# Output projection restaged: norm factor applied at each head's end, first weight chunks fetched early into idle buffers, transposes one block later

## The chip, the cores and the metric

The kernel runs on one core of a Trainium2 chip. The metric is device time in microseconds (us) of one execution. A core has a matrix engine (TensorE, "PE" in the profile, with its weight loads as "PEld"), a vector engine ("DVE"), a scalar engine for activations ("ACT"), GpSimd ("POOL"), and SyncE ("SP"), which here issues every DMA, in one order. All engines run side by side, each through its own fixed list of instructions, and wait for one another by semaphores. Data lies in DRAM, in on-chip SBUF of 128 partitions, and in PSUM banks, into which PE writes.

## The reference

A decoder trunk of two layers, 1024 tokens by 1024 features, with 256 memory tokens. Each layer projects the normalised input into the columns of several branches, mixes them into 2048 channels, gates them, and projects back with a residual:

```python
def layer(x, ...):
    u = rms_norm(x, norm_g) @ w_in          # split by columns into branches
    y = concat(branches(u)) * silu(z)       # 2048 channels
    return x + y @ w_out                    # the output projection

# layer 0: differential attention (8 heads, ALiBi), gated causal conv (512 ch.), memory attention (4 heads)
attn = p1 - lam * p2
o = einsum('bhqk,bhkd->bhqd', attn, v)
o = rms_norm(o, out_g) * (1.0 - lam_init)   # the norm factor: over a head's 128 channels, one per token
conv = b_gate * conv_w3(c_gate * h)
# layer 1: forgetting attention (12 heads) and memory attention (4 heads)
```

## The kernel before, in words

Every matrix product of the projections, of the scores and of attention with v is made of three float32r matmuls (high times high, high times low, low times high); `split` (L124) makes a high part on ACT and a low part on DVE or POOL. Tile rings decide reuse: `pool.tile(..., tag=t, bufs=n)` takes the next of the n buffers of tag t in program order, and its first writer waits until the last reader of the tile that lay there is done. A scheduler turns the program into one fixed order for each engine; two calls of `high_priority` pull attention and PSUM evacuation forward in it.

**Layer 0** runs the eight differential heads (`diff_head`, `diff_attend` L489), with a convolution group (`conv_group`, L534) spread over every two heads, then two pairs of memory heads (`x_pair`, `x_attend`), then `out_proj` (L735). Weights against the features come in two kinds: token units (`token_unit`, L187 to L191: q, k, v in token rows) and feature units (`feature_unit`, L218 to L220: gates and the convolution's four products in feature rows). Both write to the three PSUM banks of tag "d" (`pd`); scores use "s" (2), transposes "t" (2), and attention times v together with the sums of squares share one bank "o". The order lays these projections of the next head between the attention steps of this one.

In a head, `diff_attend` goes through four groups of two query blocks (`gorder` 3, 2, 1, 0): biased scores with a running maximum (L394), exponentials, e1 - lam e2 (L510 on POOL, L511 on DVE), transposes, attention times v, then y = o times gain times gate (L516), stored to `y_dr` by groups (128 KB each); the squares of o are summed by a matmul with ones (`psm`, L524) and stored as a row of `ms_dr`. At the head's end the row is loaded, `rstd` (L116, on POOL) makes the norm factor, and the factor goes to `on_dr` (L531). It is not applied there but in `out_blocks` (L702), to the stored y: four blocks of 128 channels by 128 tokens are loaded as `yr`, the factors as `rn`, broadcast over partitions, and POOL multiplies (L717).

The convolution's third product, `post_b` (L553 to L556), needs a `pd` bank and a work tile `cv` of tag "hs"; tag "hs" of pool `pa` has three buffers, used by `cv`, `zz`, `th` (the tanh of a gate), `xr` and `rs`.

`out_proj` has two halves of 512 output columns. Half 0 takes pairs of token blocks, with split weights in the buffers of u (the transposed input, no longer needed), loaded and split by the first pair; half 1 takes block after block, with weights in tiles `wo` of the pool `p2`, which were loaded during half 0. `yr`, `rn` and the raw weights share tag "raw" (4 buffers) of `pa`. At the end of each block of half 1 in layer 0 the row block of h is completed, normalised for the next layer (`norm_block`, L130) and transposed by PE into the next u (L141). Pool `p2` is opened after the branch's pools `p1` and `pw` and lies in their memory.

Of the kernel before, what the change touches and what calls it, by code (L numbers as in the profile page):

```python
# [7 lines left out]
F32 = mybir.dt.float32  # L8
F32R = mybir.dt.float32r
# [6 lines left out]
P = 128  # L16
# [17 lines left out]
class Trunk:  # L34
    def __init__(self, ctx, tc, io):
# [4 lines left out]
        self.pa = ctx.enter_context(tc.tile_pool(name="pa", bufs=1))  # L40
        self.st = ctx.enter_context(tc.tile_pool(name="st", bufs=4))
# [17 lines left out]
        self.queue, self.groups, self.boot = [], 0, True  # L59
# [70 lines left out]
    def norm_block(self, src, gb, xn, dst_hi, dst_lo):  # L130
# [5 lines left out]
        nc.vector.scalar_tensor_tensor(out=xn, in0=src, scalar=r, in1=gb, op0=ALU.mult, op1=ALU.mult)  # L136
        for j in range(2):
# [6 lines left out]
            while o < 4:  # L144
                (h, n), (l, _) = dst_hi.pop(0), dst_lo.pop(0)
                self.split(h, l, tv[:, o:o + n, :], nc.vector)
                o += n

# [29 lines left out]
    def token_unit(self, weights, lhs_hi, lhs_lo, nblk, post, together=False):  # L178
# [5 lines left out]
        for t0 in range(0, nblk, step):  # L184
# [7 lines left out]
            for tb, ps, _, _ in blks:  # L192
                with self.tc.high_priority(PRIO_EVAC):
                    post(tb, ps)
            self.tick()
# [29 lines left out]
    def gate_unit(self, w, c0, own=None):  # L225

        nc = self.nc
        if own is None:
            gate = {half: self.p1.tile([P, 512], F32, name="gate", tag="gate", bufs=2) for half in (1, 0)}
# [67 lines left out]
    def att_half(self, name):  # L297
        return self.p1.tile([P, 512], F32R, name=name, tag=name, bufs=self.attb)
# [10 lines left out]
    def mem_norm(self, layer, mem, g):  # L309
        nc = self.nc  # L310
        gb = self.p1.tile([P, T + 4], F32, name="mgb", tag="c1", bufs=1)[:, :D]
# [7 lines left out]
        for b in range(2):  # L319
            x = self.p1.tile([P, T], F32, name="mx", tag="E1", bufs=self.e1b)  # L320
            nc.sync.dma_start(out=x, in_=mem[b * P:(b + 1) * P, :])
            xn = self.p1.tile([P, T], F32, name="mxn", tag="bias", bufs=1)
# [166 lines left out]
    def diff_attend(self, h, maps, vh, vl, gate):  # L489
        nc = self.nc  # L490
        bias = self.bias
        nc.vector.tensor_scalar(out=bias, in0=bias, scalar1=0.5, scalar2=None, op0=ALU.mult)
        for g in self.gorder:
# [21 lines left out]
            y = self.pa.tile([P, 256], F32, name="y", tag="y", bufs=2)  # L515
            nc.vector.scalar_tensor_tensor(out=y, in0=o, scalar=self.g_o, in1=gate[g], op0=ALU.mult, op1=ALU.mult)  # L516
            self.emit_y(0, h, g, y)
# [13 lines left out]
        nc.sync.dma_start(out=self.on_dr[h].rearrange("(p b) -> p b", b=8), in_=self.rstd(ms, 8, "on"))  # L531


    def conv_group(self, g, w):  # L534

        nc = self.nc
        ch = self.p1.tile([P, T + 4], F32, name="ch", tag="c1", bufs=1)
# [109 lines left out]
    def fox_head(self, h, w):  # L647
# [13 lines left out]
        ck = self.p1.tile([P, T], F32, name="ck", tag="bias", bufs=1)  # L661
# [40 lines left out]
    def out_blocks(self, layer, tbs, half, tiles, res, fetch=None):  # L702
# [4 lines left out]
        for j in range(4):  # L707
            if fetch is not None:
                fetch(range(4 * j, 4 * j + 4))
            for tb, ps in zip(tbs, pss):  # L710
                ts = slice(tb * P, (tb + 1) * P)
                yr = self.pa.tile([P, 4, P], F32, name="yr2", tag="raw", bufs=4)
                nc.sync.dma_start(out=yr, in_=self.y_dr[layer][j * 512:(j + 1) * 512, ts].rearrange("(c p) t -> p c t", p=P))
                if layer == 0 and j < 2:
                    rn = self.pa.tile([P, 4, P], F32, name="rn", tag="raw", bufs=4)
                    nc.sync.dma_start(out=rn, in_=self.on_dr[4 * j:4 * j + 4, ts].unsqueeze(0).broadcast_to([P, 4, P]))
                    nc.gpsimd.tensor_tensor(out=yr, in0=yr, in1=rn, op=ALU.mult)  # L717
# [15 lines left out]
    def out_proj(self, layer, w, res, dst, g_next):  # L733
        nc, tc = self.nc, self.tc
        with tc.tile_pool(name=f"p2_{layer}", bufs=1, reuse_waits="tile") as p2:  # L735

            self.new_u()
            u = self.u
            w0 = lambda part, c: u[part][c // 8][:, c % 8, :]
            ws = [[p2.tile([P, 512], F32R, name=f"wo{p}_{c}") for c in range(16)] for p in range(2)]  # L740
            w1 = lambda part, c: ws[part][c]
            for tbs in ((tb, tb + 1) for tb in range(0, NB, 2)):
                fetch = (lambda cs: self.out_weights(w, 0, w0, cs, self.raw_tile)) if tbs[0] == 0 else None
                for tb, (ps, rs) in zip(tbs, self.out_blocks(layer, tbs, 0, w0, res, fetch)):
                    nc.vector.tensor_tensor(out=rs, in0=ps, in1=rs, op=ALU.add)
                    nc.sync.dma_start(out=dst[tb * P:(tb + 1) * P, :512], in_=rs)
                    raws = lambda: p2.tile([P, D], F32, name="wraw", tag=("hb", "xn")[tb % 2], bufs=2)[:, :512]
                    self.out_weights(w, 1, w1, range(2 * tb, 2 * tb + 2), raws)

            if g_next is not None:  # L750
                gb = p2.tile([P, D], F32, name="gb2")
                nc.sync.dma_start(out=gb, in_=g_next.broadcast_to([P, D]))
                self.new_u()
            for tb in range(NB):
                ts = slice(tb * P, (tb + 1) * P)
                hb = p2.tile([P, D], F32, name="hb", bufs=2)
                xn = p2.tile([P, D], F32, name="xn", bufs=2)
# [87 lines left out]
```

## Time and profile before

| | us |
|---|---|
| median of 3 runs | 2254.02 (2252.79 to 2254.55) |
| profiled execution, own time | 2251.72 |
| its span | 2249.9 |
| output projection 0 and the tail of the memory heads (from the last feature matmul of layer 0 to the last projection matmul) | 912.4 to 1172.0 |
| the same in layer 1 | 2053.4 to 2246.2 |

The profile is of one execution. Its page gives the busy time of each engine, the chain of work that ended last, and groups of instructions by line and shape; windows give the same between two times, and the timeline single instructions with the idle time before them and what ended it. A row such as "line engine op out<-in xcount | busy, mean ns | idle before, releaser" names the tile written, the tiles read, how often, and what the engine waited for.

### The profile page before, as it was taken

What the parts mean: (1) busy time and instruction counts of PE and PEld (TensorE: products, weight loads), DVE (VectorE), ACT (ScalarE), POOL (GpSimd) and SP (SyncE); (2) the same over time, 40 slices, a digit from 0 to 9 for tenths busy, and PEclk for the clock granted to TensorE, in tenths of its full rate; (3) what the DMA queues carried; (4) which work ended last, traced back from release to release, by engine and by line L of the source; (5) the groups of instructions that cost most, each with busy time, mean ns of one, the idle gap of its engine ahead of it and who ended that gap; (6) DMA issues with size and microseconds to landing.
All of it is one profiled execution on the core that took longest, in us unless ns stands there. A gap on an engine that the chain in (4) does not pass through costs nothing. (4 is left out here: it accounts for less than half of the span.)

```text
span 2249.9 us, 35841 instructions
## 1 busy us (share of the span) xinstructions
PE 2182.4 (97%) x12528; PEld 1974.7 (88%) x12528; DVE 1233.4 (55%) x2860; ACT 1057.8 (47%) x2503; POOL 1018.3 (45%) x1356
## 2 busy tenths in 40 slices
PE   7999999999999999888889999999999999999999
PEld 6889989889899899766679999999999999997887
DVE  5646756666665666542334555555555555555532
ACT  5655555465464554432234444444444444544421
POOL 4565655555555552332235555445555554522100
PEclk9999999999999999999999999999999999999999
DMA  5450210210201111585552221121222211214753
GB/s 162 126 159 19 61 56 17 70 47 23 71 27 44 51 59 36 168 243 161 137 144 54 57 53 36 40 55 48 55 57 57 57 40 38 61 55 137 222 155 98
DMA packets 266076, 183.06 MB, mean 81 GB/s; under 512 B 24572, under 2 KB 242844, under 8 KB 265896
## 3 DMA queue, kind: packets, MB, share of 16 engines
q1 hardware_dynamic: 265896, 180.77, 28.3%
q8 instruction: 99, 1.62, 0.3%
q14 instruction: 81, 0.66, 0.1%
HBM read 153.32 MB, written 27.38 MB: 80 GB/s over the span
## 5 line engine op out<-in xcount | busy, mean ns | idle before, releaser
L189 PE MATMUL pd<-wqh,u 128*128 128x384 f32 (+2 forms) x1536 | 513.7, 335 | 0.6 <-ACT wqh L127 0.5
L190 PE MATMUL pd<-wql,u 128*128 128x384 f32 (+2 forms) x1536 | 512.1, 334 | 0.0
L191 PE MATMUL pd<-wqh,u 128*128 128x384 f32 (+2 forms) x1536 | 511.4, 333 | 0.0
L189 PEld LDWEIGHTS pd<-wqh,u 128*128 128x128 f32 x1536 | 290.2, 189 | 4.9 <-ACT u L127 0.8
L190 PEld LDWEIGHTS pd<-wql,u 128*128 128x128 f32 x1536 | 290.2, 189 | 4.9 <-POOL wql L128 0.2
L191 PEld LDWEIGHTS pd<-wqh,u 128*128 128x128 f32 x1536 | 290.0, 189 | 4.3
L220 PE MATMUL pd<-u,wfh 128*128 128x512 f32 x704 | 277.9, 395 | 0.0
L219 PE MATMUL pd<-u,wfl 128*128 128x512 f32 x704 | 277.5, 394 | 0.0
L218 PE MATMUL pd<-u,wfh 128*128 128x512 f32 x704 | 277.2, 395 | 0.0
L128 POOL TENSOR_TENSOR wql<-raw,wqh 128x384 fp32r<-128x384 f32 (+2 forms) x220 | 217.0, 997 | 89.0 <-ACT wqh L127 83.7
L258 DVE TENSOR_TENSOR qr<-qr,rs_r 128x256 f32<-128x256 f32 x200 | 137.3, 687 | 106.7 <-POOL rs_r L121 105.2
L127 ACT ACTIVATE yh<-yr 128x512 fp32r<-128x512 f32 x128 | 79.9, 629 | 235.4 <-POOL yr L717 124.2
L121 POOL TENSOR_TENSOR rs_r<-rs_v,neghalf 128x2 f32<-128x2 f32 (+2 forms) x220 | 177.7, 809 | 14.1
L127 ACT ACTIVATE pth<-pt 128x512 fp32r<-128x512 f32 (+1 forms) x232 | 121.9, 555 | 130.1 <-PE pt L411 128.0
L673 POOL TENSOR_TENSOR fbias<-ck,cqn 128x896 f32<-128x896 f32 (+3 forms) x96 | 110.3, 1149 | 156.4 <-DVE mx L394 123.6
L128 DVE TENSOR_TENSOR yl<-yr,yh 128x512 fp32r<-128x512 f32 x128 | 89.7, 706 | 164.0 <-ACT yh L127 158.3
L127 ACT ACTIVATE wqh<-raw 128x384 fp32r<-128x384 f32 (+2 forms) x256 | 118.4, 481 | 125.4 <-DMA raw<-in_e_w_in_dram 62.6
L128 POOL TENSOR_TENSOR wfl<-rawf,wfh 128x512 fp32r<-128x512 f32 x88 | 119.4, 1358 | 106.1 <-ACT wfh L127 105.8
L128 DVE TENSOR_TENSOR ptl<-pt,pth 128x512 fp32r<-128x512 f32 (+1 forms) x232 | 143.7, 639 | 42.9 <-ACT pth L127 40.8
L128 POOL TENSOR_TENSOR vl<-qr,vh 128x128 fp32r<-128x128 f32 x160 | 80.6, 510 | 175.0 <-ACT vh L127 168.0
L220 PEld LDWEIGHTS pd<-u,wfh 128*128 128x128 f32 x704 | 132.4, 188 | 27.3 <-issue 0.6
L219 PEld LDWEIGHTS pd<-u,wfl 128*128 128x128 f32 x704 | 132.4, 188 | 26.4 <-issue 1.4
(239 smaller groups left out, 4992.4 us busy)
## 6 DMA issues: line engine op xcount, KB each, us to landing
yr<-y_dr SPq DMA_DIRECT2D x128, 256.0 KB
raw<-in_o_w_in_dram SPq DMA_DIRECT2D x288, 64.0 KB
rawf<-in_e_w_in_dram SPq DMA_DIRECT2D x56, 256.0 KB
y_dr<-y SPq DMA_DIRECT2D x112, 128.0 KB
raw<-in_e_w_in_dram SPq DMA_DIRECT2D x192, 64.0 KB
wraw<-in_e_w_out_dram SPq DMA_DIRECT2D x32, 256.0 KB
rn<-on_dr SPq DMA_DIRECT2D x32, 256.0 KB
rawf<-in_o_w_in_dram SPq DMA_DIRECT2D x32, 256.0 KB
```

Source lines behind the costliest of these rows:

```text
L121: nc.gpsimd.tensor_tensor(out=r[:, :n], in0=v[:, :n], in1=self.neghalf[:, :n], op=ALU.pow)
L127: nc.scalar.activation(out=hi, in_=src, func=AF.Copy)
L128: lo_eng.tensor_tensor(out=lo, in0=src, in1=f32(hi), op=ALU.subtract)
L189: nc.tensor.matmul(ps[:, :n], lhsT=ah(k), rhs=h, start=(k == 0), stop=False)
L190: nc.tensor.matmul(ps[:, :n], lhsT=ah(k), rhs=l, start=False, stop=False)
L191: nc.tensor.matmul(ps[:, :n], lhsT=al(k), rhs=h, start=False, stop=(k == KC - 1))
L218: nc.tensor.matmul(ps, lhsT=h, rhs=uh[:, k, :], start=(k == 0), stop=False)
L219: nc.tensor.matmul(ps, lhsT=l, rhs=uh[:, k, :], start=False, stop=False)
L220: nc.tensor.matmul(ps, lhsT=h, rhs=ul[:, k, :], start=False, stop=(k == KC - 1))
L258: nc.vector.tensor_tensor(out=v, in0=v, in1=r.unsqueeze(2).broadcast_to([P, ng, gs]), op=ALU.mult)
L673: nc.gpsimd.tensor_tensor(out=b[:, :kext], in0=ck[:, :kext], in1=self.cqn[:, qb, h:h + 1].broadcast_to([P, kext]), op=ALU.subtract)
```

## The change

Three parts.

1. The differential heads keep y of the whole head in a tile `yt` (128 channels by 1024 tokens, 2 buffers). After the factor is stored to `on_dr`, two halves of it are loaded broadcast over the partitions into `rn`, now of tag "hs"; DVE multiplies `yt` by it, and SP stores each half of y (256 KB). The 32 loads of `rn` and multiplications on POOL in `out_blocks` go.
2. A pool `pk`, open for the whole kernel, holds the tags kd, kz, c1, bias and gate. `out_early` runs ahead of the last pair of memory heads and fetches and splits the first five of 16 weight chunks of half 0 into the buffers of kd, kz (three each), c1 and bias; the other eleven go to u as before.
3. `yr` has a tag of its own (5 buffers) in `p2`; the weights of half 1 come by `raw_tile`; half 1 of layer 0 loads the first half of its row block ahead of the matmuls, and normalises it in two steps: `norm_rows` at once, `turn_rows` (the transposes) behind the next block's matmuls, the last one in the first token unit of layer 1.

```diff
+        self.pk = ctx.enter_context(tc.tile_pool(name="pk", bufs=1))
...
+            if self.turn_last is not None:
+                self.turn_last()
+                self.turn_last = None
...
-            gate = {half: self.p1.tile([P, 512], F32, name="gate", tag="gate", bufs=2) for half in (1, 0)}
+            gate = {half: self.pk.tile([P, 512], F32, name="gate", tag="gate", bufs=2) for half in (1, 0)}
...
-        return self.p1.tile([P, 512], F32R, name=name, tag=name, bufs=self.attb)
+        pool = self.pk if name in ("kd", "kz") else self.p1
+        return pool.tile([P, 512], F32R, name=name, tag=name, bufs=self.attb)
...
+        yt = self.p1.tile([P, T], F32, name="yt", bufs=2)
...
-            y = self.pa.tile([P, 256], F32, name="y", tag="y", bufs=2)
-            nc.vector.scalar_tensor_tensor(out=y, in0=o, scalar=self.g_o, in1=gate[g], op0=ALU.mult, op1=ALU.mult)
-            self.emit_y(0, h, g, y)
+            nc.vector.scalar_tensor_tensor(out=yt[:, gs], in0=o, scalar=self.g_o, in1=gate[g], op0=ALU.mult, op1=ALU.mult)
...
+        for half in range(2):
+            cs = slice(half * 512, (half + 1) * 512)
+            rn = self.pa.tile([P, 512], F32, name="rn", tag="hs", bufs=3)
+            nc.sync.dma_start(out=rn, in_=self.on_dr[h:h + 1, cs].broadcast_to([P, 512]))
+            nc.vector.tensor_tensor(out=yt[:, cs], in0=yt[:, cs], in1=rn, op=ALU.mult)
+            nc.sync.dma_start(out=self.y_dr[0][h * P:(h + 1) * P, cs], in_=yt[:, cs])
...
-        ch = self.p1.tile([P, T + 4], F32, name="ch", tag="c1", bufs=1)
+        ch = self.pk.tile([P, T + 4], F32, name="ch", tag="c1", bufs=1)
...
+    def out_early(self, w):
+
+        early = [[], []]
+        for i in range(3):
+            for part, n in enumerate(("kd", "kz")):
+                early[part].append(self.att_half(n))
+        for t in ("c1", "bias"):
+            two = self.pk.tile([P, T + 4] if t == "c1" else [P, T], F32R, name="we", tag=t, bufs=1)
+            for part in range(2):
+                early[part].append(two[:, part * 512:(part + 1) * 512])
+        self.early = early
+        self.out_weights(w, 0, lambda part, c: early[part][c], range(len(early[0])), self.raw_tile)
...
-    def out_blocks(self, layer, tbs, half, tiles, res, fetch=None):
+    def out_blocks(self, layer, tbs, half, tiles, res, pool, fetch=None):
...
-                yr = self.pa.tile([P, 4, P], F32, name="yr2", tag="raw", bufs=4)
+                yr = pool.tile([P, 4, P], F32, name="yr2", tag="yr", bufs=5)
...
-                if layer == 0 and j < 2:
-                    rn = self.pa.tile([P, 4, P], F32, name="rn", tag="raw", bufs=4)
-                    nc.sync.dma_start(out=rn, in_=self.on_dr[4 * j:4 * j + 4, ts].unsqueeze(0).broadcast_to([P, 4, P]))
-                    nc.gpsimd.tensor_tensor(out=yr, in0=yr, in1=rn, op=ALU.mult)
...
-            u = self.u
-            w0 = lambda part, c: u[part][c // 8][:, c % 8, :]
+            u, early = self.u, self.early
+            ne = len(early[0])
+            w0 = lambda part, c: early[part][c] if c < ne else u[part][(c - ne) // 8][:, (c - ne) % 8, :]
...
-                fetch = (lambda cs: self.out_weights(w, 0, w0, cs, self.raw_tile)) if tbs[0] == 0 else None
-                for tb, (ps, rs) in zip(tbs, self.out_blocks(layer, tbs, 0, w0, res, fetch)):
+                fetch = (lambda cs: self.out_weights(w, 0, w0, [c for c in cs if c >= ne], self.raw_tile)) if tbs[0] == 0 else None
+                for tb, (ps, rs) in zip(tbs, self.out_blocks(layer, tbs, 0, w0, res, p2, fetch)):
...
-                    raws = lambda: p2.tile([P, D], F32, name="wraw", tag=("hb", "xn")[tb % 2], bufs=2)[:, :512]
-                    self.out_weights(w, 1, w1, range(2 * tb, 2 * tb + 2), raws)
+                    self.out_weights(w, 1, w1, range(2 * tb, 2 * tb + 2), self.raw_tile)
...
+            turn = None
...
-                xn = p2.tile([P, D], F32, name="xn", bufs=2)
-                ((ps, rs),) = self.out_blocks(layer, [tb], 1, w1, res)
+                if g_next is not None:
+                    nc.sync.dma_start(out=hb[:, :512], in_=dst[ts, :512])
+                ((ps, rs),) = self.out_blocks(layer, [tb], 1, w1, res, p2)
+                if turn is not None:
+                    turn()
                 nc.vector.tensor_tensor(out=hb[:, 512:], in0=ps, in1=rs, op=ALU.add)
                 nc.sync.dma_start(out=dst[ts, 512:], in_=hb[:, 512:])
                 if g_next is not None:
-                    nc.sync.dma_start(out=hb[:, :512], in_=dst[ts, :512])
-                    self.norm_block(hb, gb, xn, *self.u_dst(tb))
+                    t = ("bias", "c1")[tb % 2]
+                    xn = self.pk.tile([P, T + 4] if t == "c1" else [P, T], F32, name="xn2", tag=t, bufs=1)[:, :D]
+                    self.norm_rows(hb, gb, xn)
+                    turn = lambda xn=xn, tb=tb: self.turn_rows(xn, *self.u_dst(tb))
+            self.turn_last = turn
...
+                if pr == 1:
+                    self.out_early(io["e_w_out"][0])
```

What this does to the lists of instructions, at three places. The lines of "after" are twelve to eighteen numbers higher for the same code (L516 is L529, L553 to L556 are L571 to L574, L524 is L536, L218 to L220 are L230 to L232).

DVE at the third odd head (of eight, counted from 0, the head 5), before, around the first scores of head 5 (`e_7271` and `e_7272`; the y is head 4's last):

```order
L295 TENSOR_TENSOR kz<-pt,kd 64x256
L553 TENSOR_SCALAR cv<-ch,cw,cb 128x512 x2
L394 ISA e_7271,mxp<-pss,abias 128x512
L394 ISA mxp 128x1
L554 SCALAR_TENSOR_TENSOR cv<-ch,cw,cv 128x512 x2
L394 ISA e_7272,mxp<-pss,abias 128x512
L394 ISA mxp 128x1
L555 SCALAR_TENSOR_TENSOR cv<-ch,cw,cv 128x512 x2
L516 SCALAR_TENSOR_TENSOR y<-po,g_o,gate 128x256
L242 SCALAR_TENSOR_TENSOR gate<-th,pd 128x512
L394 ISA e_7271,mx<-pss,abias,mxp 128x384
L394 ISA mx 128x1
```

DVE in the changed kernel, at the end of head 5:

```order
L525 SCALAR_TENSOR_TENSOR e_7638<-e_7638,rl,e_7639 128x256
L529 SCALAR_TENSOR_TENSOR yt<-po,g_o,gate 128x256
L129 TENSOR_TENSOR ptl<-pt,pth 128x384
L529 SCALAR_TENSOR_TENSOR yt<-po,g_o,gate 128x256
L571 TENSOR_SCALAR cv<-ch,cw,cb 128x512
L572 SCALAR_TENSOR_TENSOR cv<-ch,cw,cv 128x512
L548 TENSOR_TENSOR yt<-yt,rn 128x512
L573 SCALAR_TENSOR_TENSOR cv<-ch,cw,cv 128x512
L548 TENSOR_TENSOR yt<-yt,rn 128x512
L571 TENSOR_SCALAR cv<-ch,cw,cb 128x512
L574 TENSOR_TENSOR ch<-cv,pd 128x512
```

The convolution's `cv` stood between the two heads and ahead of the scores of head 5; it now stands at the end of head 5, and the product that frees a `pd` bank (`ch<-cv,pd`) behind the two multiplications by `rn`.

PE before, around the last sum of squares (`psm`) of head 5; `u` and `wfh` or `wfl` are feature units, `pss` scores of the next head:

```order
L220 MATMUL pd<-u_99,wfh 128x512
L218 MATMUL pd<-u_97,wfh 128x512
L219 MATMUL pd<-u_97,wfl 128x512
L524 MATMUL psm<-sqh,ones_r 2x256
L220 MATMUL pd<-u_99,wfh 128x512
L218 MATMUL pd<-u_97,wfh 128x512
L219 MATMUL pd<-u_97,wfl 128x512
L525 MATMUL psm<-sql,ones_r 2x256
L220 MATMUL pd<-u_99,wfh 128x512
L218 MATMUL pd<-u_97,wfh 128x512
L219 MATMUL pd<-u_97,wfl 128x512
L377 MATMUL pss<-kh,qh 128x512
```

PE in the changed kernel, at the same sum:

```order
L424 MATMUL pt<-ident,e_7638 128x128 x2
L536 MATMUL psm<-sqh,ones_r 2x256
L537 MATMUL psm<-sql,ones_r 2x256
L436 MATMUL po<-pth,vh 128x256
L437 MATMUL po<-pth,vl 128x256
L438 MATMUL po<-ptl,vh 128x256
L436 MATMUL po<-pth,vh 128x128
L437 MATMUL po<-pth,vl 128x128
L438 MATMUL po<-ptl,vh 128x128
L536 MATMUL psm<-sqh,ones_r 2x256
L537 MATMUL psm<-sql,ones_r 2x256
L230 MATMUL pd<-u_100,wfh 128x512
L231 MATMUL pd<-u_100,wfl 128x512
```

Feature matmuls stood between all steps of the attention; now those steps follow each other, and 24 feature matmuls and then the 192 projection matmuls of the next head come behind the last sum.

SP before, at the start of output projection 0; `y` is the memory heads' and `yr`, `rn`, `rs`, `wraw` the projection's:

```order
L429 DMA y_dr_72<-y 128x256 x7
L696 DMA wraw<-in_e_w_out_dram 128x512
L585 DMA xr<-xm_75 128x512
L429 DMA y_dr_72<-y 128x256
L713 DMA yr_11793<-y_dr_72 128x4x128
L716 DMA rn<-on_dr 128x4x128
L713 DMA yr_11814<-y_dr_72 128x4x128
L716 DMA rn<-on_dr 128x4x128
L729 DMA rs<-in_x_dram 128x512 x2
L696 DMA wraw<-in_e_w_out_dram 128x512
L729 DMA rs<-in_x_dram 128x512
L696 DMA wraw<-in_e_w_out_dram 128x512 x3
```

SP in the changed kernel, at the same place:

```order
L714 DMA wraw<-in_e_w_out_dram 128x512 x2
L442 DMA y_dr_75<-y 128x256
L714 DMA wraw<-in_e_w_out_dram 128x512 x2
L442 DMA y_dr_75<-y 128x256 x6
L744 DMA yr_11816<-y_dr_75 128x4x128
L744 DMA yr_11834<-y_dr_75 128x4x128
L744 DMA yr_11864<-y_dr_75 128x4x128
```

The first load of `yr` stood among the last stores of y, with one or more y still to come; now it stands behind all of them. On PE the first matmul of the projection (L724) stood between scores and transposes of the memory heads' last iterations; now (L751) it stands behind the last matmul of attention times v.

21 lines of the change are left out of this document (14 added, 7 removed).

## The prediction

> **What bounds the kernel now.** I read the page's totals first, then its chain, then the waits of PE in each stage.
>
> ```profile
> span 2249.9 us, 35841 instructions
> PE 2182.4 (97%) x12528; PEld 1974.7 (88%) x12528; DVE 1233.4 (55%) x2860; ACT 1057.8 (47%) x2503; POOL 1018.3 (45%) x1356
> PE 46%; DMA 1%; DVE 1%; issue 0%; ACT 0%; POOL 0%; ACTq 0%; POOLq 0%; SPq 0%
> ```
>
> PE (matmul) is busy for 97% of the span, and the chain that ended last is almost all PE. So an edit can gain only what PE now waits, 2249.9 - 2182.4 = 67.5 us, and half clock; it can lose any amount, wherever PE's fixed order runs out of work that is ready. Where do the 67.5 us lie? By windows (the columns are the busy us of each engine, then granted clock, DMA share, GB/s) and by PE's waits (us in total, times, longest) in the stretch 912.39 to 1172:
>
> ```profile
> core 0: us, PE busy (x) PEld busy (x) DVE busy (x) ACT busy (x) POOL busy (x), PEclk, DMA share, GB/s
> 582.77:673.00 90.23, 90.23 (x514) 81.89 (x513) 60.36 (x145) 48.95 (x121) 50.46 (x61) 1.00 0.16 48
> 912.39:1172.00 259.61, 220.00 (x926) 173.58 (x925) 99.02 (x165) 81.77 (x158) 70.84 (x66) 0.92 0.61 175
> 2053.40:2246.20 192.80, 190.30 (x870) 155.41 (x868) 84.15 (x145) 65.64 (x124) 18.56 (x14) 1.00 0.55 170
> ```
>
> ```profile
> PE pd L724 <- ACT yh L127: 22.6, 9, 4.1
> PE pt L141 <- DVE xn L136: 14.4, 6, 4.1
> PE pd L726 <- DVE yl L128: 2.6, 3, 1.3
> ```
>
> The first window is the attention of one odd differential head (its first score to its last y): PE never idles. The second is layer 0's output projection with the tail of the memory heads: 39.6 us idle and a mean clock of 0.92. The third is the same in layer 1: 2.5 us idle. So the change has about 40 us to win in layer 0's projection, nothing in layer 1's, and nothing in the heads.
>
> **Part one: the norm factor at each head's end.** It takes 32 multiplications and 32 loads off the projection:
>
> ```profile
> L717 POOL TENSOR_TENSOR yr<-yr,rn 128x512 f32<-128x512 f32 x32 | 41.9, 1309 | 151.7 <-DMA rn<-on_dr 125.5 <-DMA yr<-y_dr 16.2 <-issue 5.3
> ```
>
> POOL's 41.9 us are not on the path by themselves; their wait for `rn` delays yh, which is the 22.6 us above. In exchange each head ends with two `rn` loads, two multiplications on DVE and two stores. Price of these alone: 16 x 0.68 us = 11 us of DVE, hidden if DVE has slack. What matters is the ring: `rn` takes two of the three "hs" buffers, in program order ahead of the `cv` that the convolution allocates next. In the order of before, DVE computes both `cv` at the start of an odd head (the x2 row of L553 among the rows of the change, ahead of the first score); in the order of after they stand behind the head's last y, because the second `cv` needs a buffer that `rn` frees. PE's feature matmuls need one of three "d" banks, and a bank is freed by `ch<-cv,pd`. So PE has three banks of feature matmuls (72 of 512 columns) and then nothing but the head's own attention; the next head's 192 projection matmuls, which used to be woven in, come behind, bare.
>
> How long is that stretch? In the third odd head PE's order, from the head's first score to the place where feature work resumes, holds 234 matmuls: 72 of features and 162 of attention. Two 512-column matmuls start 0.22 to 0.23 us apart:
>
> ```profile
> 911.12 0.39 PE L219 MATMUL pd<-u,wfl 128*128 128x512 f32 x1
> 911.34 0.39 PE L220 MATMUL pd<-u,wfh 128*128 128x512 f32 x1
> ```
>
> At that pace the columns of the 234 make 34.6 us, 18 of them attention. Against this stands the chain. Rows of 200 to 800 us (seven heads less one group: 27 groups, 53 to 54 blocks):
>
> ```profile
> L394 DVE CUSTOM_DVE_ANT_0 e<-pss,abias 128x512 f32<-128x512 f32 (+3 forms) x107 | 62.0, 587 | 30.4 <-PE pss L377 18.7 <-PE pt L411 11.0
> L511 DVE SCALAR_TENSOR_TENSOR e<-e,rl,e 128x512 f32<-128x512 f32 (+7 forms) x54 | 57.5, 1066 | 16.1 <-POOL e L510 15.8
> L128 DVE TENSOR_TENSOR ptl<-pt,pth 128x512 fp32r<-128x512 f32 (+1 forms) x67 | 40.8, 632 | 12.6 <-ACT pth L127 11.6
> L394 DVE CUSTOM_DVE_ANT_0 e<-pss,abias,mxp 128x384 f32<-128x384 f32 (+3 forms) x56 | 30.4, 545 | 18.2 <-PE pss L377 17.9
> L509 DVE TENSOR_TENSOR rl<-rl,lam 128x1 f32<-128x1 f32 x53 | 14.5, 273 | 1.1
> L503 DVE TENSOR_SCALAR nm<-mx 128x2 f32<-128x2 f32 x53 | 14.3, 271 | 1.5
> L516 DVE SCALAR_TENSOR_TENSOR y<-po,g_o,gate 128x256 f32<-128x256 f32 x27 | 13.0, 482 | 4.2 <-PE po L425 3.3
> L508 DVE RECIPROCAL rl<-ls 128x2 f32<-128x2 f32 x53 | 8.6, 162 | 37.3 <-ACT e L506 37.1
> L394 DVE DVE_READ_ACCUMULATOR2_ANT mx<- 128x1 f32 x106 | 8.5, 80 | 0.0
> L554 DVE SCALAR_TENSOR_TENSOR cv<-ch,cw,cv 128x512 f32<-128x512 f32 x8 | 9.1, 1181 | 0.0
> L555 DVE SCALAR_TENSOR_TENSOR cv<-ch,cw,cv 128x512 f32<-128x512 f32 x8 | 6.1, 797 | 0.0
> L556 DVE TENSOR_TENSOR ch<-cv,pd 128x512 f32<-128x512 f32 x8 | 5.4, 680 | 0.0
> L553 DVE TENSOR_SCALAR cv<-ch,cw,cb 128x512 f32<-128x512 f32 x8 | 4.0, 544 | 0.1
> ```
>
> Per head (four groups, eight blocks): scores (62.0 + 30.4) x 4/27 + 24 reads x 0.08 = 15.6; `e` 57.5 x 8/54 = 8.5; `ptl` ten x 0.61 = 6.1; small ones (14.5 + 14.3 + 8.6) x 8/53 = 5.6; y 1.9; two gates, the bias and the even head's two `rn` multiplications, priced like L556, five x 0.68 = 3.4. DVE's own work up to the last y is 41 us, which is the floor. The ceiling is the same head in before, woven with other work: 582.77 to 673, 90 us.
>
> ```profile
> 582.77 0.69 DVE L394 CUSTOM_DVE_ANT_0 e<-pss,abias 128x512 f32<-128x512 f32 x1
> 625.21 0.48 DVE L516 SCALAR_TENSOR_TENSOR y<-po,g_o,gate 128x256 f32<-128x256 f32 x1 [0.61 <-PE po L425]
> ...
> 672.90 0.48 DVE L516 SCALAR_TENSOR_TENSOR y<-po,g_o,gate 128x256 f32<-128x256 f32 x1
> 682.08 0.25 SPq L528 DMA_DIRECT2D ms_dr<-osq  x1
> 683.19 0.35 SPq L530 DMA_DIRECT2D on_ms<-ms_dr  x1
> 688.64 0.33 SPq L531 DMA_DIRECT2D on_dr<-on_r  x1
> ```
>
> I take 64: the first group is a chain of its own (42 us from score to y in before; 40 here), and the other three then run at DVE's pace, about 24 of its rows' us, since PE no longer has other work ahead of theirs. Behind the last y stand its square, psm and the `ms` store, 4.5 us (9.2 in before, among other work); 1.1 to the load of `on_ms`; 5.5 to the store of `on_dr`; 1.1 again to the `rn` load, which I take to wait for its store as `on_ms` does; and the landing of 256 KB with its hop, 3.5 us, by these rows:
>
> ```profile
> 2041.12 0.43 SPq L585 DMA_DIRECT2D xr<-xm  x1
> 2044.64 0.63 ACT L127 ACTIVATE vh<-xr 128x512 fp32r<-128x512 f32 x1 [2.92 <-DMA xr<-xm]
> ```
>
> Then DVE's fixed row of `yt<-yt,rn`, L555, `yt<-yt,rn`, L553, L556: 0.68 + 0.80 + 0.68 + 0.54 + 0.68 = 3.4. Sum 64 + 4.5 + 1.1 + 5.5 + 1.1 + 3.5 + 3.4 = 83 against 35 of matmuls: **48 us of idle PE**. Bounds: with DVE's floor of 41 in place of 64 it is 25; with the last three groups half way between 24 us and the 48 they took in before (625.21 to 673), 60. All four odd heads have this order; the first has 48 more feature matmuls (11 us) beside it, so 3 x 48 + 37 = **181**, between 89 and 229. I hold to the walk, because it takes each step from the row of the same instruction.
>
> SP's queue is moved too: at each head's end two stores wait for DVE's multiplications, and the next heads' weight loads stand behind them, some 5 us later than before (3.5 of landing and two times 0.68). PE now waits for weights in the heads for
>
> ```profile
> PE pd L189 <- ACT wqh L127: 1.8, 2, 1.3
> ```
>
> in the whole run, so they come early and I price this at nothing; without that cover it is 8 x 5 = 40 us at most.
>
> **Part two: early weights and `yr` in the projection's pool.** The order shows the first `yr` load behind the last y stores of the memory heads, and PE's first projection matmul behind the last pv matmul: `yr` now lies in memory that the attention's buffers held. In before `yr` sat in a pool of its own, and projection and tail were woven (912.39 above is that point). The tail, eight iterations, now runs bare:
>
> ```profile
> 861.89 22.43 SPq L429 DMA_DIRECT2D y_dr<-y  x7
> 917.30 0.80 PE L724 MATMUL pd<-u,yh 128*128 128x512 f32 x1 [4.12 <-ACT yh L127]
> ...
> 920.67 0.63 PE L726 MATMUL pd<-u,yl 128*128 128x512 f32 x1
> 921.10 0.63 PE L724 MATMUL pd<-u,yh 128*128 128x512 f32 x1
> ...
> 923.23 0.41 PE L726 MATMUL pd<-u,yl 128*128 128x512 f32 x1
> ```
>
> Seven y in 22.4 us, so 3.7 each: eight take 29 us, in which PE has 10 us of matmuls. (The floor is PE's 10; the ceiling 40, with a weight split as long as L717's 1.31 in each.) Then 3.5 for the first `yr`, 0.6 for yh, and a start at half rate: after the wait of 4.12 us the matmuls start 0.43 us apart until about 922.8, 5.5 us in which 2.6 are lost. Together 36 us. What remains is the projection. Layer 1's window gives it at clock 1.00: 190.3 busy less the tail's 10 = 180; layer 0 has 64 transposes more, 5 us. Layer 0: 36 + 185 = 221 instead of 259.6, **-39** (-58 to -28): the wait for yh is gone with the multiplications, that for xn with the transposes' delay, and with the gaps the half clock. Layer 1 had nothing to win: 36 + 180 = 216 instead of 192.8, **+23** (4 to 34). The early weights cost nothing by themselves: their ten splits lie beside the last x_pair's matmuls; what they save is part of the 39.
>
> Sum against the profiled execution (2251.72 us, 1.8 more than its span): 2251.7 + 181 - 39 + 23 = 2417. The median of the runs, 2254.02, lies 2.3 above that execution, so 2419.
>
> **The rivals.** (1) *The ring does not decide.* If `cv` and the feature matmuls need not wait for `rn`, or the chain is shorter than the 35 us of matmuls, only part two is left: 2254 - 39 + 23 = 2238, faster. For it: PE never idled in 582.77 to 673, and its total work is unchanged. Against: the order puts `ch<-cv,pd` behind both `yt<-yt,rn`, and DVE's own rows are 41 us. 0.07. (2) *Only the round trip shows.* The groups keep pace with PE, and just the 19 us behind the last y stand bare, four times: 2254 + 76 - 16 = 2314. For it: in before the groups were slowed by woven work. Against: between two groups the order has no more than three banks of it. 0.12. (3) *PE turns cold in the stretches.* By the rows of 917 to 923 a wait of 4 us costs half rate for 5.5 us, and the stretches are full of such waits. Then the 162 attention matmuls, 18 us, take 36; if half to all of that lies on the chain, 4 x 9 to 4 x 18 come on top: 2455 to 2491, at the middle 2473. Against: DVE's rows lead, not PE's. 0.12. (4) Gains and losses meet within 0.2%: 0.02. My forecast, 2419 (2345 to 2455): 0.67.
>
> The Trainium skill, "TensorE: Matmul & The Clock Gate", section "Part 1: The HAM clock gate", puts the drop to half rate at one idle window of about 3.4 us; the 4.12 us wait above agrees. It speaks against this change, and by it rival 3 would hold wherever the stretches' waits are longer than that.
>
> The range, 2325 to 2480, takes in the bounds of the stretch and of the tail, and with them most of rivals 2 and 3. About 0.2% (4.5 us) is what a measurement of this kernel can tell from no change. Faster 0.07, same 0.02, slower 0.91.
>
> **What would show it.** In the trace of the changed kernel: four gaps in PE of 35 to 60 us near the ends of the odd heads, with PE's `pd` matmuls waiting for DVE's `ch` and DVE for the DMA of `rn`; PE's slices there at 4 to 7 tenths; projection 0 near 221 us from the last feature matmul, projection 1 near 216, its first matmul waiting for `yr`; no `rn` wait on POOL. If PE's slices stay at 9 between 200 and 800 us, the part on the ring is wrong; if projection 1 still takes 193, the part on the pool is.

## The result, and the profile after

| | before | changed |
|---|---|---|
| median, us (runs) | 2253.4 (2251.18 to 2254.55, 4) | 2429.75 (2420.33 to 2434.44, 4) |
| ratio of the changed kernel to before, 95% interval | | 1.0779 [1.0745, 1.0812] |
| profiled execution, its own time | 2251.72 | 2430.37 |

The change makes the kernel 7.8% slower. The page of the changed kernel, its totals and slices:

```profile
span 2428.6 us, 35784 instructions
PE 2241.9 (92%) x12528; PEld 2007.3 (83%) x12528; DVE 1239.5 (51%) x2876; ACT 1064.6 (44%) x2503; POOL 960.6 (40%) x1324
PE   7899699869986996798999999999999999998999
PEclk9999799969987997899999999999999999998999
```

PE has the same 12528 matmuls, is busy for 60 us longer and idle for 187 us where it was idle for 67. A slice is 60.7 us. Four dips stand in the slices 5, 8 to 9, 12 to 13 and 16 to 17, all in layer 0's heads, and the granted clock dips in the same places; two smaller ones, 19 and 37, are the starts of the projections. Line numbers are those of the changed kernel: its L146 (transposes of `xn`) is L141 of before, its L751 to L753 (projection matmuls) are L724 to L726. What PE waited for in the whole run (us in total, times, longest), the first rows:

```profile
PE pd L230 <- DVE ch L574: 52.5, 4, 13.4
PE pt L424 <- DVE e L525: 23.1, 13, 6.3
PE psm L536 <- ACT sqh L128: 18.4, 14, 2.0
PE pt L146 <- DVE xn L137: 14.1, 2, 9.9
PE pd L751 <- ACT yh L128: 10.5, 2, 5.7
```

Four times, once at each odd head, a feature matmul (L230) waits some 13 us for `ch<-cv,pd`; the next two rows are waits inside the attention, which in before had other matmuls beside it. The end of head 3, the second odd head, in the timeline, DVE and then SP:

```profile
516.23 0.48 DVE L529 SCALAR_TENSOR_TENSOR yt<-po,g_o,gate 128x256 f32<-128x256 f32 x1 [2.31 <-PE po L438]
516.63 0.54 DVE L571 TENSOR_SCALAR cv<-ch,cw,cb 128x512 f32<-128x512 f32 x1
...
528.75 0.69 DVE L548 TENSOR_TENSOR yt<-yt,rn 128x512 f32<-128x512 f32 x1 [10.79 <-DMA rn<-on_dr]
529.36 0.74 DVE L573 SCALAR_TENSOR_TENSOR cv<-ch,cw,cv 128x512 f32<-128x512 f32 x1
530.02 0.69 DVE L548 TENSOR_TENSOR yt<-yt,rn 128x512 f32<-128x512 f32 x1
530.62 0.54 DVE L571 TENSOR_SCALAR cv<-ch,cw,cb 128x512 f32<-128x512 f32 x1
531.08 0.68 DVE L574 TENSOR_TENSOR ch<-cv,pd 128x512 f32<-128x512 f32 x1
```

```profile
519.40 0.21 SPq L540 DMA_DIRECT2D ms_dr<-osq  x1
520.49 0.35 SPq L542 DMA_DIRECT2D on_ms<-ms_dr  x1
524.19 0.35 SPq L543 DMA_DIRECT2D on_dr<-on_r  x1
525.61 0.79 SPq L547 DMA_DIRECT2D rn<-on_dr  x2
```

DVE stands 10.8 us before the first multiplication by `rn`, because `ms`, `on_ms`, `on_dr` and `rn` go through DRAM one after the other. The product that frees a bank comes behind it. On PE, the head's first score and the feature matmul that waits for this product:

```profile
449.12 0.39 PE L390 MATMUL pss<-kh,qh 128*128 128x512 f32 x1
...
531.82 0.80 PE L230 MATMUL pd<-u,wfh 128*128 128x512 f32 x1 [12.85 <-DVE ch L574]
```

From the one to the other the stretch took 82.7 us. Windows over it, over the 25 us behind it, and over the same stretch of head 5, the head whose order the prediction counts (busy us by engine, granted clock, DMA share, GB/s):

```profile
449.12:531.82 82.70, 50.78 (x236) 39.36 (x234) 41.26 (x111) 30.28 (x72) 29.50 (x33) 0.76 0.16 49
531.82:557.00 25.18, 25.18 (x124) 23.48 (x125) 8.68 (x15) 5.68 (x14) 7.76 (x11) 0.89 0.14 46
674.75:757.65 82.90, 50.31 (x236) 38.99 (x234) 41.48 (x110) 30.02 (x71) 29.10 (x33) 0.78 0.16 49
```

For 32 us of head 3's stretch PE was idle. The 50.8 us in which it worked are 42 us at full clock (busy time times granted clock, added up over windows of 1 us; the mean of 0.76 covers idle time too), so the slow clock costs 9 us here, and by the second row 3 more behind the stretch. Head 5 gives the same within 1 us. To see the whole program, I cut it in four at the start of the last feature matmul of a layer and of the last projection matmul. For the changed kernel these are the following rows of the timeline, with the first projection matmul of each layer between:

```profile
1104.16 0.40 PE L232 MATMUL pd<-u,wfh 128*128 128x512 f32 x1
1132.15 0.79 PE L751 MATMUL pd<-kd,yh 128*128 128x512 f32 x1 [4.82 <-ACT yh L128]
1317.25 0.40 PE L753 MATMUL pd<-wo,yl 128*128 128x512 f32 x1
2213.19 0.40 PE L232 MATMUL pd<-u,wfh 128*128 128x512 f32 x1
2244.64 0.79 PE L751 MATMUL pd<-kd,yh 128*128 128x512 f32 x1 [5.66 <-ACT yh L128]
2424.43 0.40 PE L753 MATMUL pd<-wo,yl 128*128 128x512 f32 x1
```

In before the cuts lie at 911.34, 1171.77, 2052.35 and 2245.79. The same cuts of every run (differences of such rows, us of each profiled execution; equal parts of two runs differ by up to 3.5 us, as those of `part1` and `hs5` or of `best` and `late` do):

| run | layer 0 to last feature matmul | tail and projection 0 | heads of layer 1 | tail and projection 1 |
|---|---|---|---|---|
| before | 911.3 | 260.4 | 880.6 | 193.4 |
| changed | 1104.2 | 213.1 | 895.9 | 211.2 |
| yt_one | 1100.9 | 214.3 | 896.5 | 208.4 |
| rn_own | 928.0 | 215.1 | 895.2 | 210.7 |
| cv_own | 1015.0 | 213.9 | 897.3 | 209.2 |
| yr_raw | 1102.3 | 210.1 | 883.8 | 201.6 |
| both | 927.1 | 210.1 | 884.5 | 201.3 |
| rn_y_yr | 940.9 | 209.8 | 884.6 | 201.8 |
| part23 | 916.3 | 262.3 | 896.6 | 208.2 |
| part1 | 1095.9 | 197.1 | 880.2 | 192.8 |
| hs5 | 1099.4 | 197.7 | 880.5 | 191.9 |
| best | 921.0 | 198.3 | 880.0 | 192.6 |
| late | 923.2 | 198.6 | 880.3 | 193.9 |
| no_mult | 912.6 | 257.1 | 879.6 | 191.6 |

The changed kernel loses 192.9 us in layer 0's heads, wins 47.3 in projection 0, and loses 15.3 and 17.8 in layer 1.

### The profile page after: what moved, and what is told of

Same layout as the page of the kernel before. It is cut to its first block, busy times and chain, and to the rows that moved or that the text cites. A ratio compares the mean times of both kernels' runs of the same rounds, so it can differ in the third digit from the quotient of the medians.

```text
span 2428.6 us, 35784 instructions
## 1 busy us (share of the span) xinstructions
PE 2241.9 (92%) x12528; PEld 2007.3 (83%) x12528; DVE 1239.5 (51%) x2876; ACT 1064.6 (44%) x2503; POOL 960.6 (40%) x1324
## 4 chain that ended last, share of the span: by engine, by line
PE 79%; DMA 6%; DVE 5%; POOL 4%; ACT 3%; issue 2%; SPq 1%; POOLq 0%; ACTq 0%; DVEq 0%
PE pd L198 10%; PE pd L199 10%; PE pd L200 10%; PE pd L230 6%; PE pd L231 6%; PE pd L232 6%; PE pss L390 6%; PE pd L751 5%; PE pd L752 5%; PE pd L753 5%; PE pt L424 3%; PE po L438 2%; PE po L437 2%; PE po L436 2%; PE pt L279 1%
## 5 line engine op out<-in xcount | busy, mean ns | idle before, releaser
L230 PE MATMUL pd<-u,wfh 128*128 128x512 f32 x704 | 285.7, 406 | 58.3 <-DVE ch L574 52.5
L231 PE MATMUL pd<-u,wfl 128*128 128x512 f32 x704 | 283.6, 403 | 0.9 <-POOL wfl L129 0.9
L232 PE MATMUL pd<-u,wfh 128*128 128x512 f32 x704 | 282.5, 401 | 0.0
L230 PEld LDWEIGHTS pd<-u,wfh 128*128 128x128 f32 x704 | 136.3, 194 | 87.2 <-DVE ch L574 53.6
L128 ACT ACTIVATE pth<-pt 128x512 fp32r<-128x512 f32 (+1 forms) x232 | 122.2, 557 | 156.5 <-PE pt L424 154.1
L128 ACT ACTIVATE yh<-yr 128x512 fp32r<-128x512 f32 x128 | 80.8, 631 | 232.2 <-PE pd L752 214.6
L128 ACT ACTIVATE wqh<-raw 128x384 fp32r<-128x384 f32 (+2 forms) x256 | 117.9, 480 | 106.5 <-DMA raw<-in_e_w_in_dram 47.5
L232 PEld LDWEIGHTS pd<-u,wfh 128*128 128x128 f32 x704 | 136.0, 193 | 28.7 <-issue 0.3
```

The source lines that it names most:

```text
L128: nc.scalar.activation(out=hi, in_=src, func=AF.Copy)
L230: nc.tensor.matmul(ps, lhsT=h, rhs=uh[:, k, :], start=(k == 0), stop=False)
L231: nc.tensor.matmul(ps, lhsT=l, rhs=uh[:, k, :], start=False, stop=False)
L232: nc.tensor.matmul(ps, lhsT=h, rhs=ul[:, k, :], start=False, stop=(k == KC - 1))
```

## The experiments

**Is it the ring of `rn`?** First a control, since `rn` needs room of its own and one of yt's two buffers pays for it.

```diff
-        yt = self.p1.tile([P, T], F32, name="yt", bufs=2)
+        yt = self.p1.tile([P, T], F32, name="yt", bufs=1)
```

> Control for the next run: yt with one buffer instead of two, and nothing else. The order of PE's matmuls around the odd heads' ends stays as in the changed kernel. Every theory expects the time of the changed kernel, 2430 us within 10; if the second buffer of yt mattered, some 10 to 40 us more.

Measured: 2426.49 us, ratio to before 1.0748 [1.0724, 1.0773]. The buffer doesn't matter. Then the ring:

```diff
-        yt = self.p1.tile([P, T], F32, name="yt", bufs=2)
+        yt = self.p1.tile([P, T], F32, name="yt", bufs=1)
-            rn = self.pa.tile([P, 512], F32, name="rn", tag="hs", bufs=3)
+            rn = self.p1.tile([P, 512], F32, name="rn", bufs=2)
```

> The changed kernel with rn in a tag of its own (two buffers, paid for by one buffer of yt instead of two), so that it takes nothing of the ring hs; the loads, multiplications and stores at each head's end stay. Theory (the ring): the four bare stretches go, PE's windows from 200 to 800 us are full again, no wait of pd matmuls for ch; 2430 less the 193 us that layer 0 lost up to its last feature matmul = 2237 to 2250. Rival (the round trip at each head's end costs time whatever the ring): 15 us stay at each of four heads, 2300. Rival (the order of the heads is not the cause at all): 2430.

Measured: 2254.7 us, 0.9991 [0.998, 1.0002]; the table shows 928.0 against 1100.9 of the control. PE's slices of this run, and its window at the place of the stretch above:

```profile
PE   7899999999999999899989999999999999998999
PEclk9999999999999999999999999999999999998999
```

```profile
450.00:550.00 100.00, 99.82 (x577) 91.03 (x576) 59.42 (x154) 54.76 (x134) 53.26 (x68) 1.00 0.15 43
```

The same loads, multiplications and stores, with the same round trip through DRAM, cost 172 us less (2426.49 to 2254.7) when `rn` lies outside the ring. The rival of the round trip (2300) falls. The time is above the 2237 to 2250 that I gave: the heads kept 17 us over before.

**Which user of the ring?** `cv` outside, `rn` inside:

```diff
-            c = self.pa.tile([P, 512], F32, name="cv", tag="hs", bufs=3)
+            c = self.p1.tile([P, 512], F32, name="cv", bufs=2)
```

(and yt with one buffer).

> The changed kernel with cv, not rn, in a tag of its own (two buffers, yt with one); rn, th and zz stay in the ring hs. It tells which user of the ring blocks. If the convolution's cv alone holds the pd banks: as with rn in its own tag, 2255. If th and zz, which also free pd banks and stand behind rn, block as much: 2426. I expect that both count, and that the bare stretches get shorter: 2300 (2280 to 2340).

Measured: 2342.27 us, 1.039 [1.0376, 1.0404], half way between the control and `rn_own`: 1015.0 against 1100.9 and 928.0, and just above the range that I gave. With `cv` outside, half of the loss goes, and with it PE's wait for `ch` (0.3 us in the whole run). The other half was not pinned to one user: `th`, the tanh that takes a buffer of the same ring, still waits for the reader of `rn`, but for less than in the changed kernel. First the changed kernel, then this run, in ACT's waits:

```profile
ACT th L253 <- DVE yt L548: 49.3, 6, 11.9
ACT th L253 <- DVE yt L548: 14.8, 4, 7.4
```

**Is it a matter of the number of buffers?** Part one alone is described below; this is part one with a longer ring:

```diff
-            rn = self.pa.tile([P, 512], F32, name="rn", tag="hs", bufs=3)
+            rn = self.pa.tile([P, 512], F32, name="rn", tag="hs", bufs=5)
```

(the same for the other users of the tag, and yt with one buffer).

> Part one alone with rn left in the ring hs, which now has five buffers instead of three (yt with one). If the number of buffers that rn takes is what counts (two of three), five cure it: 2200. If the place in the ring counts, the tanh of the convolution's gate, the fifth buffer after rn, still waits for it; the order still shows the bare stretches: 2371 less at most 20, so 2350 to 2372. I expect the latter.

Measured: 2370.89 us, 1.0513 [1.0499, 1.0527], against 2371.06 with three buffers: two more bought nothing. DVE in the timeline of this run, at the end of head 3:

```profile
516.54 1.00 DVE L558 TENSOR_SCALAR cv<-ch,cw,cb 128x512 f32<-128x512 f32 x2
529.06 0.69 DVE L535 TENSOR_TENSOR yt<-yt,rn 128x512 f32<-128x512 f32 x1 [9.73 <-DMA rn<-on_dr]
...
530.33 0.69 DVE L535 TENSOR_TENSOR yt<-yt,rn 128x512 f32<-128x512 f32 x1
...
531.60 0.68 DVE L242 SCALAR_TENSOR_TENSOR zz<-th,pd 128x512 f32<-128x512 f32 x1
532.19 1.28 DVE L561 TENSOR_TENSOR ch<-cv,pd 128x512 f32<-128x512 f32 x2
```

and PE's wait:

```profile
532.33 0.79 PE L218 MATMUL pd<-u,wfh 128*128 128x512 f32 x1 [13.13 <-DVE zz L242]
```

Now both `cv` start ahead of `rn`, and `zz` stands behind it. I had named the tanh; it ran on ACT at 519.52, and ACT's waits of this run have no row of `th` for `yt` any more, so it is the product of `zz`, behind both multiplications in DVE's order, that is late. The loss thus stays without the wait for the ring's buffer that `th` showed above: what counts here is DVE's fixed order. The order also leaves `cv` at the head's end, though two of five buffers should have been free earlier; why the scheduler put it there stays open.

**What does each part do alone?** Part one on the kernel before (`rn` in "hs" with three buffers, as in the change):

> The kernel before with part one alone: y kept in yt, rn loaded into the ring hs at each head's end, no rn and no POOL multiplication in the projection; no early weights, yr in raw, transposes as before. Theory (the ring makes the whole loss of the heads): up to the last feature matmul of layer 0 some 1102 us as in the changed kernel (911 before), and 20 to 30 us less in projection 0: 2254 + 191 - 25 = 2420 (2405 to 2435). Rival (the loss needs part two, such as the new pool's tags): 2230 to 2300.

Measured: 2371.06 us, 1.0523 [1.0506, 1.0539]. The heads lose what they lose in the changed kernel (1095.9), but projection 0 takes 197.1, which is 63 less than before and 16 less than in the changed kernel, and layer 1 is as before. PE's waits in projection 0 of this run are a single row:

```profile
PE pd L725 <- ACT yh L127: 0.4, 1, 0.4
```

My expectation was wrong in the size, 25 for 63. And the changed kernel without part one:

> The changed kernel without part one: norm factor applied in the projection by POOL as before, early weights, yr in pool p2 and late transposes as changed. Theory: heads of layer 0 as before (911 us up to the last feature matmul), projection 0 some 20 us over the changed kernel's 213, the part between the projections and projection 1 as in the changed kernel (896 and 211): 2253 (2245 to 2265). If the 17 us that rn in its own tag still lost in the heads come from the new pool and not from part one: 2270.

Measured: 2287.08 us, 1.0144 [1.013, 1.0159], more than both values that I gave. The heads are within 5 us of before, so the new pool costs little there; but projection 0 wins nothing (262.3), with these waits:

```profile
PE pd L750 <- ACT yh L128: 18.4, 7, 6.2
PE pt L146 <- DVE xn L137: 16.1, 5, 6.4
```

The transposes, though a block later, still wait for `xn` here, and in `part1`, where they come at once, they wait for nothing.

**Loads or multiplications?** On the kernel before:

```diff
-                    nc.gpsimd.tensor_tensor(out=yr, in0=yr, in1=rn, op=ALU.mult)
+                    nc.gpsimd.tensor_tensor(out=yr[:, 0, :1], in0=yr[:, 0, :1], in1=rn[:, 0, :1], op=ALU.mult)
```

> The kernel before, with the multiplication by the norm factor in the projection cut from 512 columns to one, so the factor is left out of the other 511; loads of rn, ring raw and all waits stay. If POOL's 1.31 us a piece delays yh: projection 0 falls from 260 to some 215, 2210. If the loads and their ring delay it: it stays above 245, 2240 to 2254. I expect the loads: 2246.

Measured: 2250.48 us, 0.9981 [0.9972, 0.999], and projection 0 at 257.1. The group on POOL:

```profile
L717 POOL TENSOR_TENSOR yr<-yr,rn 128x1 f32<-128x1 f32 x32 | 6.5, 204 | 184.0 <-DMA rn<-on_dr 162.2 <-issue 10.4 <-DMA y_dr<-y 7.5
```

A piece takes 0.20 us instead of 1.31, and POOL waits longer for `rn` instead (162 us, 125.5 in before). So POOL's working time is at most 3 of the 63 us. The other 60 go with the 32 loads, their buffers in the ring "raw", their place in SP's queue and the extra step over POOL, which this run still has; these were not tried apart.

**Where does `yr` belong?**

```diff
-                yr = pool.tile([P, 4, P], F32, name="yr2", tag="yr", bufs=5)
+                yr = self.pa.tile([P, 4, P], F32, name="yr2", tag="raw", bufs=4)
```

> The changed kernel with yr back in the ring raw of pool pa (four buffers, shared with the raw weights), all else as changed: the projections' first matmuls are again woven into the tails of the memory heads. Theory (placement of yr): projection 1 loses its 19 us, back to about 193 from the last feature matmul; projection 0 wins up to 28 us (wait from the last feature matmul to the first projection matmul) less what the shared ring costs: 2385 to 2410. Rival (the tail's bareness is due to the early weights, or is hidden): 2430.

Measured: 2402.32 us, 1.0637 [1.0616, 1.0659]: 3 less in projection 0, 12 less in the heads of layer 1, 10 less in projection 1. The first projection matmul now starts 0.2 us behind the last feature matmul in both layers, yet the projections stay 13 and 9 us over `part1`; each has one long wait for yh, 5.6 us in projection 1 and in projection 0 this one (window 1102 to 1313):

```profile
PE pd L751 <- ACT yh L128: 9.0, 1, 9.0
```

What causes these waits was not tried. The placement is real but worth less than I gave it. With `rn` in its own tag as well:

> Both edits of the two runs before: rn in a tag of its own and yr in raw. The theories add: 2430 - 190 - 35 = 2205 (2195 to 2225), faster than the kernel before. If the two edits share their gain, 2240.

Measured: 2226.77 us, 0.9862 [0.9843, 0.988]. The gains add (172 and 28 us), and the kernel is faster than before by 1.4%. It lies just above the range that I gave, because `rn` gave 172 for the 190 that I took and `yr` 28 for 35.

**Another place for `rn`**: four quarters of 256 columns in the ring "y", with yt at two buffers and `yr` in "raw".

> A version meant to keep both gains: the changed kernel with rn in four quarters in the ring y (two buffers of 256 columns, next used only by the next head's first group), yt with two buffers, and yr in raw. Theory: 2227 of the run with both edits, less what the single buffer of yt costs in the heads (up to 12 us): 2215 to 2227, so 1.3 to 1.8% faster than the kernel before. If the four small loads cost more than they give: 2235.

Measured: 2244.82 us, 0.996 [0.9946, 0.9974]. A miss: 18 us more than `both` by the medians, 14 in the profiled executions, all of them in the heads (940.9). PE there waits for DVE's scores (150 to 941 us):

```profile
PE pss L390 <- DVE mxp L407: 14.7, 6, 4.1
```

**The version that beats both.** Part one on the kernel before, with `rn` in its own tag and one buffer of yt; parts two and three left out.

> The kernel before with part one alone, but rn in a tag of its own (two buffers, yt with one); parts two and three left out. Theory: heads of layer 0 some 11 us over before (rn_own was 17 over, part23 5 over without part one), projection 0 197 us as in the run of part one alone (260 before), the rest as before: 922 + 197 + 880 + 193 + 6 = 2198 (2190 to 2212), the fastest so far. Rival (part one's gain in projection 0 needs the heads' lateness, since the loads are then long done): 2235.

Measured: 2201.65 us, 0.9764 [0.975, 0.9777], 2.4% faster than before. The page:

```profile
PE 2162.1 (98%) x12528; PEld 1963.0 (89%) x12528; DVE 1248.6 (57%) x2876; ACT 1059.8 (48%) x2503; POOL 975.1 (44%) x1324
PE   7899999999999999999999999999999999999999
```

DVE still waits for `rn`, at most 5.6 us at a time, but PE has other work meanwhile:

```profile
DVE yt L535 <- DMA rn<-on_dr: 32.4, 10, 5.6
```

On it the late transposes alone:

```diff
-                    self.norm_block(hb, gb, xn, *self.u_dst(tb))
+                    self.norm_rows(hb, gb, xn)
+                    turn = (lambda xn=xn, tb=tb: self.turn_rows(xn, *self.u_dst(tb)))
+            if turn is not None:
+                turn()
```

(and `turn()` of the block before, behind a block's matmuls).

> The run best with the transposes of half 1 one block later (the last ones at the projection's end), and nothing else of parts two and three. Theory (once the loads of rn are gone, projection 0 has nothing left to wait for): the same as best within 4 us. Rival (late transposes are worth the 14 us of waits for xn that the profile of before showed): 10 us less than best.

Measured: 2200.93 us, 0.9756 [0.9743, 0.9769]. No difference: there was nothing left to hide.

## Why the prediction was right, and where its terms were off

The time (2419 for 2430) and the sign were right, and the cause named first, `rn` in the ring "hs", is the one that the runs show: with three buffers the heads lose their time, and a tag for `rn` alone gives nearly all of it back, in the changed kernel (`rn_own`) and in part one alone (`best` against `part1`). That the total came so near is in part luck. By the profiled executions the change cost 179 us for the 165 foretold: two terms that I had put at nothing cost 17 and 15, and the other three each came out lower than foretold, by 5, 8 and 5.

- **The ring, +181: right, measured +176** (1104.2 less the 928.0 of `rn_own`). The waits are those foretold: PE for `ch`, DVE for `rn`, at each of the four odd heads. The walk gave 83 us from the first score to the resumed feature matmul; head 3 took 82.7 and head 5 82.9. Its steps were off by little: in head 3 the first y came 39 us after DVE's first score (40 foretold), the last y 27.5 after that (24), and PE resumed 15.6 later (19). The matmuls beside it were mis-sized: counted by columns 35 us, they are 42 at full clock, and they ran slower than that. So "48 us of idle PE" was 32 of idle and, with what follows behind the stretch, 11 of slow clock. Over all of layer 0's heads PE was idle for 123 us more than in `rn_own` and busy for 54 more with as many matmuls; first the changed kernel, then `rn_own`:

```profile
0.00:1104.16 1104.16, 952.45 (x5285) 841.28 (x5286) 570.97 (x1352) 512.36 (x1248) 471.92 (x621) 0.92 0.19 58
0.00:927.97 927.97, 898.86 (x5286) 814.79 (x5286) 576.98 (x1352) 506.26 (x1248) 485.15 (x621) 0.99 0.23 70
```

The third rival's condition, a cold clock, thus held, but not its price: the stretches are no longer than the walk, so the slow matmuls took time in which PE would have waited. The four gaps were smaller (27 to 34 us of idle each) than the 35 to 60 that I gave as the sign.
- **One link of the ring is not shown.** I had `cv` stand at the head's end because it needs a buffer that `rn` frees. In `hs5` there are two buffers more, both `cv` start ahead of `rn`, `th` no longer waits for it, and the loss is the same, with `zz` in the place of `ch`. That `rn` must not lie in this ring is shown; what puts the users of the ring at the head's end is not.
- **The heads without the ring: priced at nothing, measured 17.** 5 of them appear without part one (`part23`), 10 with part one alone in its best form (`best`, 921.0). By the windows of `rn_own` and before (911.34 us: 890.12 busy), 8 are more idle time of PE and 9 more busy time; which of the added instructions makes them was not separated.
- **Projection 0, -39: near the measured -47, for the wrong reasons in part.** I credited part one with the waits for yh, the late transposes with those for `xn`, and charged the bare tail to the same sum. Part one alone gives -63 and takes both waits away; parts two and three give +2 alone and +16 on top of part one. The step that failed is that the wait for `xn` goes "with the transposes' delay": the 14.4 us fell with the loads of `rn`, and `late` shows nothing for the delay. That the clock comes back with the gaps held: 0.98 in the changed kernel, 1.00 in `part1`.
- **The bare tail, 33 us to the first projection matmul (29 + 3.5 + 0.6), and what it costs:** in projection 0 there were 28.0 us from the last feature matmul to the first of the projection (1104.16 to 1132.15), in projection 1 31.5, so the tail's size was about right. Projection 1 lost 18 (23 foretold). But the gap is not the whole cause: with it closed (`yr_raw`) projection 0 fell by 3 us only and projection 1 by 10. What in parts two and three makes the rest was not shown.
- **Missed: 15 us in the heads of layer 1.** No step had it. 12 of them lie in the first 51 us behind projection 0 (39 in before, up to the same feature matmul): waits for `xn` (4.1) and for `qr` (3.6), and a clock of 0.93 instead of 1.00. `rn_own` has the same; with `yr` in "raw" as well (`both`) the waits are gone, the clock is 1.00 and the stretch takes 40 us. How the place of `yr` brings them about was not shown.
- **The opposite rival** (2238, if the ring didn't decide) is near what `rn_own` came to, 2255: the 17 and the 15 that I had put at nothing came on top, and the projections came out some 12 us better than foretold.

## What to carry to other kernels

A tile taken from a shared ring has a place in program order, and whoever takes the next turn waits for its release, whatever the priorities say; before giving a long-lived tile, one that waits for a round trip through memory, a place in a ring of short-lived ones, look at who comes next in it and whether that one frees a PSUM bank. A longer ring needn't help, since the engine's fixed order can keep the wait when the buffers no longer do (`hs5`); another tag did, with the same memory in all. Split a change of several parts before judging it: here one part was worth 53 us (2255.07 to 2201.65) once freed of its ring, and the other two only took from it.

## What the runs showed that was not expected

The clock fell without long waits. In the stretch of head 3 these two waits were the longest between 503 and 516 us:

```profile
504.62 0.28 PE L536 MATMUL psm<-sqh,ones_r 128*2 128x256 f32 x1 [1.08 <-ACT sqh L128]
506.14 1.06 PE L424 MATMUL pt<-ident,e 128*128 128x128 f32 x5 [1.25 <-DVE e L525]
```

and in the windows around them (PE's busy time first, granted clock third from the end) the clock, just back at full rate, goes to half rate again:

```profile
502.00:504.00 2.00, 1.54 (x9) 1.34 (x8) 1.15 (x7) 1.39 (x7) 0.95 (x4) 0.73 0.00 0
504.00:506.00 2.00, 0.28 (x1) 0.08 (x1) 0.99 (x3) 0.54 (x2) 2.00 (x4) 1.00 0.00 0
506.00:508.00 2.00, 1.27 (x6) 0.77 (x6) 1.97 (x8) 1.19 (x4) 0.67 (x1) 0.62 0.00 0
...
510.00:512.00 2.00, 2.00 (x10) 1.61 (x9) 0.88 (x2) 0.00 (x0) 0.42 (x1) 0.50 0.00 0
```

The Trainium skill, "TensorE: Matmul & The Clock Gate", section "Part 1: The HAM clock gate", names one idle window of about 3.4 us for the drop. The 4.12 us wait in before agrees with that. Here the clock fell after two waits of little over a microsecond with 0.28 us of work between them, so 2.3 us of 2.6 idle; whether the half rate just before helped was not tested.

The same instruction of DVE took another time by its place. The convolution's second step, 1.18 us in before (L554 above), is in the changed kernel, where it runs at a head's end:

```profile
L572 DVE SCALAR_TENSOR_TENSOR cv<-ch,cw,cv 128x512 f32<-128x512 f32 x8 | 6.0, 749 | 0.1
```

In `best`, where it is back among the scores, it takes 1.27 us. In before and in `best` POOL works on the low parts of weights beside it (in before POOL's L128 from 229.21 to 232.10 us, DVE's two steps from 228.74 to 231.22); in the changed kernel's head 3 POOL is idle when it starts (517.21) and takes up an operation at 517.66. Whether that slows it was not tested.
